# Layer norms of a two-layer hybrid decoder step without GpSimd, with an earlier shift, six blocks in the first group and one pool of PSUM banks

## The chip, the cores and the metric

The kernel runs on one core of one Trainium2 chip. The metric is the time of one execution on the device in microseconds (us). The engines are named as the profile names them: PE (TensorE, the matrix products; PEld is its weight load), DVE (VectorE), ACT (ScalarE), POOL (GpSimd) and SP (SyncE, which issues DMAs).

## The reference

One inference step of 320 tokens (256 of a prompt, 8 sequences of 8) through two layers. Each layer is

```python
h = LayerNorm(alpha * x + W_out [GDN(x) | DiffAttn(x) | GLA(x)])
x = LayerNorm(alpha * h + SwiGLU(h))
# _layer_norm:
mu = jnp.mean(xf, -1, keepdims=True)
var = jnp.mean(jnp.square(xf - mu), -1, keepdims=True)
return ((xf - mu) * lax.rsqrt(var + eps) * g + b)
```

D_MODEL is 2048, so a layer norm runs over 16 blocks of 128 features. The three mixers (gated delta rule, differential attention with a paged cache, gated linear attention) take their columns from one input projection. All tensors are fp32, and the dense products are kept near fp32 by splitting both operands.

## The kernel before

**Layout.** Activations are feature-major: 128 features on the partitions, 320 tokens in the free dimension, 16 blocks `m` for the 2048 features. `acc(m)` (line 766) is the fp32 sum of block `m`; its blocks lie in `blkB`, `accq` and `sv`. `xh` and `xl` hold the input of the next product as high and low part.

**Dense products.** Weights come in units of 256 KB, `raw` (128 x 512), by DMA from SP. ACT casts each to its high part `whi` (`conv_hi`), DVE subtracts to get the low part `wlo` (`conv_lo`), four units ahead. One unit holds four 128 x 128 tiles, and each tile is three products on PE: `whi` by `xh`, `whi` by `xl`, `wlo` by `xh`. So a unit is 12 products, and an output block over 16 k-blocks is 48. There are 19392 dense products in all. A layer has, in this order: the input projection (54 blocks in the order of `IN_BLOCKS`, and the small block `sm` with gates), the output projection in two halves of its inputs (`hf` 0 and 1, 16 blocks each), and the SwiGLU in three parts (gate and up blocks, then 16 `dn` blocks per part). The second half, and the third part, add to `acc(m)`.

**Layer norm.** `ln_part` (line 1070) runs when a block of the last half or part is done. For the first four blocks POOL sums them into `c`, a product with a constant turns that into a mean over 512 features, and `c` is subtracted from every block on DVE as a shift near the mean. `ln_acc` then forms the square on ACT, adds block and square to `S1` and `S2` on POOL, and writes g times the block into `xh` and `xl`. The next product starts on these before the statistics are known: `four` (line 894) makes the first four output blocks go together, one k-block at a time over four banks, with two more columns (322 instead of 320) that carry -g and b; their correction follows in `block_value`. Meanwhile `ln_task` takes two products with a constant for mean and mean square, then the reciprocal root `r`, and then for each block subtracts mu on POOL (`ln_scale`), multiplies by `r` on DVE, applies g and b on ACT twice (`xh` and `acc`) and forms `xl` on DVE. A block may be overwritten only when the first group has used its k-block. The fifth output block needs all of them. There are four layer norms: two feed a SwiGLU, one feeds the input projection of layer 1, and the last (`ln_out`, line 1185) writes the result `y`.

**Banks.** PSUM has 8 banks. Banks 0 to 2 (printed as bank_79 to bank_81) are for dense blocks, 3 to 7 (bank_82 to bank_86) for the mixers; a dense block takes a mixer bank only when no dense bank is free in the program as written.

**What sets the order.** The operations are recorded and then put in an order by `Program.order` (line 511), which knows costs and latencies of each engine, keeps dependencies and the order of the dense products, and takes on each engine the operation with the longest tail behind it. The engines then run their lists in order and wait for one another by semaphores. The planner's costs do not include that DVE and POOL slow each other.

Line 671 of the profile is the call that issues every recorded operation, so rows are told apart by tile names. `geng` and `gen` are the memories that temporaries come from (`c`, `S1`, `S2`, squares and corrected blocks among them).

Of the kernel before, what the change touches and what calls it, by code (L numbers as in the profile page):

```python
# [120 lines left out]
class Mem:  # L121
    """columns of one SBUF tile handed out and taken back in program order, longest-free or (fit) smallest first"""
# [58 lines left out]
class Clock:  # L181
    """rough engine times, used only to choose the order in which work is issued"""
# [56 lines left out]
class TagTile:  # L239
    """a tile of a tag, made when its turn comes in the final order"""  # L240
# [5 lines left out]
class LazyAP:  # L246
    """access pattern of a TagTile: a stand-in for shapes, and the steps that lead to the real one"""
# [53 lines left out]
def region(ap):  # L301
    """(memory, first and last partition, [(first column, last column)]) of an access pattern"""
# [38 lines left out]
class Program:  # L341
    """operations as they are asked for, put in another order that keeps what they depend on, then issued"""
# [6 lines left out]
    # ---- dependencies  # L349
# [19 lines left out]
    def epoch(self, key):  # L369
        """a bank begins a new use"""  # L370
# [51 lines left out]
    def _merge(self, g, o, reads, writes, quads):  # L422
        """o runs beside g, in other columns of the array"""
# [86 lines left out]
    # ---- order  # L510
    def order(self):
# [42 lines left out]
        while len(res) < len(ops):  # L554
# [15 lines left out]
            # choose  # L570
# [103 lines left out]
def aps_of(name, a, kw):  # L674
    """(read, written) access patterns of an operation"""
# [43 lines left out]
def emit(nc, pool, psp, T, O, coff, ioff, n_pages):  # L719
# [32 lines left out]
    dense_free = deque(range(ND))  # L752
    mix_free = deque(range(ND, 8))
# [9 lines left out]

    def acc(m):
# [8 lines left out]
    # ---------------------------------------------------------------- helpers  # L773
# [20 lines left out]
    def rsqrt_small(out, v):  # L794
        """out = v ** -0.5 for a few columns"""
# [6 lines left out]
    # ---------------------------------------------------------------- tasks  # L802
# [63 lines left out]
    def bank(n=1):  # L866
        if clk.task.t > clk.t["PE"] + SLACK:
            yield
        while len(mix_free) < n:
            yield WAIT  # L870
        bs = [mix_free.popleft() for _ in range(n)]
# [4 lines left out]
    def fb(*bs):  # L876
        for b in bs:
            mix_free.append(b)
# [9 lines left out]
    # ---------------------------------------------------------------- units  # L888
# [5 lines left out]
    def four(W, u, keys, ln):  # L894
        """four output blocks, all of them one k at a time; x is not normalized yet where ln is given"""
        for k in range(KB):
            mms = [(keys[m], k, m * 128, k == 0, k == KB - 1) for m in range(4)]
            units.append(dict(src=W[u + k], mms=mms, x=xs2 if ln else xs, n=NT + 2 if ln else NT,
                              pre=("ln" if ln else "x", ln, k)))
        lazy.update({keys[m]: ln for m in range(4) if ln})  # L900

    def one(W, u, key, nk, x, pre=None):
        """one output block over nk k-blocks, four at a time"""
# [5 lines left out]
    def in_units(l):  # L909
# [3 lines left out]
        four(W, 0, keys, ln)  # L913
        u = KB
        for m in range(4, len(keys)):
            u = one(W, u, keys[m], KB, xs, ("h", ln) if ln and m == 4 else None)
            if m == 4:
# [10 lines left out]
    def ffn_units(l):  # L928
        W, W2 = T["wgu"][l], T["wd"][l]
        u = d = 0  # L930
        for pi, (f0, nf) in enumerate(FPARTS):
            keys = [("gu", l, f, gu) for f in range(f0, f0 + nf) for gu in range(2)]
            ms = 0
            if pi == 0:
                four(W, 0, keys, (l, 0))
                u, ms = KB, 4
            for m in range(ms, len(keys)):
                u = one(W, u, keys[m], KB, xs, ("h", (l, 0)) if pi == 0 and m == 4 else None)
# [26 lines left out]
    # ---------------------------------------------------------------- weight stream  # L965
# [1637 lines left out]
```

## Time and profile before

| | |
|---|---|
| median of 3 runs | 3383.41 us (3383.02 to 3388.16) |
| span of the profiled execution | 3386.1 us |
| PE busy | 3292.8 us (97%) |
| DVE busy | 1976.8 us (58%) |
| ACT busy | 1484.9 us (44%) |
| POOL busy | 596.7 us (18%) |
| mean granted TensorE clock | 0.990 |

The time of the profiled execution is not among the three given apart from its span; the span lies 2.7 us above the median and inside the range of the runs. Products overlap (a row of 0.31 us starts 0.15 us after the one ahead), so the pace of PE is read from starts and counts, not from durations. A row with xN joins N like instructions that follow one another.

### The profile page before, as it was taken

How to read it: one execution, taken by the hardware profiler on the slowest of the kernel's cores; microseconds unless marked ns; L12 is line 12 of the kernel's file. 1: busy time of each engine (PE TensorE's matmuls, PEld its weight loads, DVE VectorE, ACT ScalarE, POOL GpSimd, SP SyncE). 2: the span in 40 equal slices, each digit the busy share in tenths (PEclk: the TensorE clock that was granted, in tenths of full speed). 3: DMA queues.
4: the chain of work that ended last, by engine and by line, in shares of the span. 5: the costliest groups of instructions: out<-in, count | busy, mean ns of one | idle time of the engine just before them, and what ended most of it. 6: DMA issues, size and time to landing. Idle time of an engine off the chain costs nothing. (4 is left out here: it accounts for less than half of the span.)

```text
span 3386.1 us, 70352 instructions
## 1 busy us (share of the span) xinstructions
PE 3292.8 (97%) x26570; PEld 3101.2 (92%) x26570; DVE 1976.8 (58%) x3624; ACT 1484.9 (44%) x3059; POOL 596.7 (18%) x825
## 2 busy tenths in 40 slices
PE   9999999999999999999999999999899999999996
PEld 8888787889999999999988887878899999999996
DVE  6666448786445444444876664587954454444446
ACT  5444444445433443344564443453644334433443
POOL 0233423260000000000523333231600000000005
PEclk9999999999999999999999999999999999999998
DMA  6455753434454554544444567434344545454443
GB/s 217 140 175 184 243 189 123 138 118 147 150 150 150 151 150 150 150 150 150 146 145 139 177 213 242 155 116 153 118 147 150 150 150 152 151 150 150 150 150 109
DMA packets 264696, 527.89 MB, mean 156 GB/s; under 512 B 31394, under 2 KB 33570, under 8 KB 264226
## 3 DMA queue, kind: packets, MB, share of 16 engines
q1 hardware_dynamic: 243874, 456.26, 43.8%
q0 software_dynamic: 20480, 67.13, 6.0%
q8 instruction: 208, 3.41, 0.4%
q14 instruction: 134, 1.10, 0.1%
HBM read 506.25 MB, written 16.36 MB: 154 GB/s over the span
## 5 line engine op out<-in xcount | busy, mean ns | idle before, releaser
L671 DVE TENSOR_TENSOR wlo<-raw,whi 128x512 fp32r<-128x512 f32 x1616 | 1166.8, 723 | 1152.9 <-PE bank L671 950.9
L671 ACT CAST whi<-raw 128x512 fp32r<-128x512 f32 x1616 | 999.7, 620 | 1443.2 <-PE bank L671 1351.1
L671 PE MATMUL bank<-xh,whi 128*128 128x320 f32 (+1 forms) x4544 | 1423.0, 313 | 22.3 <-DVE geng L671 10.3
L671 PE MATMUL bank<-xh,wlo 128*128 128x320 f32 (+1 forms) x4544 | 1424.4, 313 | 7.6 <-DVE wlo L671 7.6
L671 PE MATMUL bank<-xl,whi 128*128 128x320 f32 (+1 forms) x4544 | 1420.9, 313 | 0.1
L671 PEld LDWEIGHTS bank<-xh,whi 128*128 128x128 f32 x4544 | 860.4, 189 | 37.9 <-DVE geng L671 11.1
L671 PEld LDWEIGHTS bank<-xh,wlo 128*128 128x128 f32 x4544 | 862.5, 190 | 15.7 <-DVE wlo L671 10.1
L671 PEld LDWEIGHTS bank<-xl,whi 128*128 128x128 f32 x4544 | 860.3, 189 | 15.5 <-issue 11.8
L671 POOL TENSOR_TENSOR geng<-blkB 128x320 f32<-128x320 f32 x8 | 8.1, 1009 | 1747.8 <-DVE blkB L671 1747.8
L671 PE MATMUL bank<-actA,whi 128*128 128x320 f32 x1152 | 254.9, 309 | 0.0
L671 PEld LDWEIGHTS bank<-actA,whi 128*128 128x128 f32 x1152 | 192.7, 188 | 0.0
L671 PE MATMUL bank<-actA,wlo 128*128 128x320 f32 x576 | 177.9, 309 | 0.0
L671 PE MATMUL bank<-actB,whi 128*128 128x320 f32 x768 | 171.2, 310 | 0.0
L671 PE MATMUL bank<-actCh,whi 128*128 128x320 f32 x448 | 138.4, 309 | 0.0
L671 PE MATMUL bank<-actCl,whi 128*128 128x320 f32 x448 | 138.4, 309 | 0.0
L671 PE MATMUL bank<-actCh,wlo 128*128 128x320 f32 x448 | 138.4, 309 | 0.0
L671 PEld LDWEIGHTS bank<-actB,whi 128*128 128x128 f32 x768 | 128.6, 188 | 0.6
L671 PE MATMUL bank<-actB,wlo 128*128 128x320 f32 x384 | 118.9, 310 | 0.1
L671 PE MATMUL bank<-geng,gen 128*32 128x256 f32 (+5 forms) x968 | 109.0, 468 | 5.7 <-DMA geng<-in_ck 4.9
L671 PEld LDWEIGHTS bank<-actA,wlo 128*128 128x128 f32 x576 | 108.3, 188 | 0.0
L671 PEld LDWEIGHTS bank<-g 32*32 32x32 f32 (+2 forms) x2784 | 56.1, 111 | 40.4 <-issue 34.6
L2003 POOL DMA_DIRECT2D geng<-in_cvp x128 | 69.4, 542 | 121.4 <-PE bank L671 100.7
(297 smaller groups left out, 3621.8 us busy)
## 6 DMA issues: line engine op xcount, KB each, us to landing
raw<-in_wgu SPq DMA_DIRECT2D x704, 256.0 KB
raw<-in_win SPq DMA_DIRECT2D x434, 256.0 KB
raw<-in_wd SPq DMA_DIRECT2D x352, 256.0 KB
geng<-in_ck POOLq DMA_DIRECT2D x128, 256.0 KB, 3.9
geng<-in_cvp POOLq DMA_DIRECT2D x128, 256.0 KB, 3.8
raw<-in_wout SPq DMA_DIRECT2D x128, 256.0 KB
c<-in_sgdn SPq DMA_DIRECT2D x6, 512.0 KB
out_gs<-c SPq DMA_DIRECT2D x6, 512.0 KB
```

The source lines that it names most:

```text
L671: fn(*[real(x) for x in a], **{k: real(v) for k, v in kw.items()})
L2003: G.eng.dma_start(out[:, k * 512:k * 512 + 512], src[l, ds(reg, 1)].rearrange(pat))
```

## The change

- The shift moves one part ahead: `ln_shift` runs in the last half but one or part but one (output projection: half 0; SwiGLU: part 1), and `ln_part` in the last one finds blocks that are already shifted.
- All sums and subtractions of the layer norms go from POOL to DVE. `ln_scale`, and the difference for `xl`, work on two blocks at once (128 x 640), and so does the output: `ln_out` uses DVE for both steps, ACT for all 16 affine steps, and 8 DMAs of 320 KB.
- The first group has six output blocks instead of four (`first` instead of `four`, 24 units instead of 16); two `dk` blocks move into it, and the small block comes behind the seventh block instead of the fifth.
- Outside the stretch from the small block to the second half of the output projection (`widen`), all eight banks are one pool that is taken in turn, for dense blocks and mixers alike.

```diff
+FIRST = 6
 IN_BLOCKS = (
     [("dv", h) for h in range(4)]
+    + [("dk", h) for h in (2, 3)]
     + HALF[0]
     + [("dq", h) for h in range(4)]
-    + [("dk", h) for h in range(4)]
+    + [("dk", h) for h in (0, 1)]
...
-    dense_free = deque(range(ND))
-    mix_free = deque(range(ND, 8))
+    dense_free, mix_free = deque(range(8)), deque()
+    wide = [True]
+
+    def widen(on):
+        wide[0] = on
+        old = list(dense_free) + list(mix_free)
+        dense_free.clear()
+        mix_free.clear()
+        for b_ in old:
+            free_dense(b_)
...
     def free_dense(bi):
-        if bi < ND:
+        if wide[0] or bi < ND:
             dense_free.append(bi)
...
+    def first(W, u, keys, ln):
+        todo = [(k, m) for k in range(KB) for m in range(FIRST)]
+        for q in range(len(todo) // 4):
+            km = todo[4 * q:4 * q + 4]
+            mms = [(keys[m], k, i * 128, k == 0, k == KB - 1) for i, (k, m) in enumerate(km)]
...
+            else:
+                widen(True)
...
         if "sm" in u:
+            widen(False)
             small_block(i, u["sm"])
...
+    def ln_shift(ln, m):
+        st = LN
+        if m == 0:
+            st.clear()
+            st["c"] = al(NT)
+            return
         c = ap(st["c"])
         if m < 4:
             if m == 1:
-                tt(G, c, acc(0), acc(1), ALU.add)
+                tt(V, c, acc(0), acc(1), ALU.add)
             elif m > 1:
-                tt(G, c, c, acc(m), ALU.add)
+                tt(V, c, c, acc(m), ALU.add)
             if m == 3:
...
                 for mm_ in range(4):
-                    ln_acc(ln, mm_)
+                    tt(V, acc(mm_), acc(mm_), c, ALU.subtract)
         else:
-            ln_acc(ln, m)
+            tt(V, acc(m), acc(m), c, ALU.subtract)
...
-        tt(V, a, a, c, ALU.subtract)
...
-                tt(G, S1, S1, a, ALU.add)
-            tt(G, S2, S2, sq, ALU.add)
+                tt(V, S1, S1, a, ALU.add)
+            tt(V, S2, S2, sq, ALU.add)
...
-    def ln_scale(m, e):
-        """t -> (t - mu) r"""
-        a = acc(m)
-        tt(e, a, a, ap(LN["S1"]), ALU.subtract)
-        tt(V, a, a, ap(LN["S2"]), ALU.mult)
+    def ln_scale(m):
+        a = acc2(m)
+        for s, op in (("S1", ALU.subtract), ("S2", ALU.mult)):
+            tt(V, a, a, ap(LN[s])[:, None, :].to_broadcast([128, 2, NT]), op)
...
+        for q in (m, m + 1):
+            g, b = pv(l, o + q, 1), pv(l, o + 16 + q, 1)
+            A.activation(xh[:, q, 0:NT], acc(q), AF.Identity, scale=g, bias=b)
+            A.activation(acc(q), acc(q), AF.Identity, scale=g, bias=b)
+        tt(V, xl[:, m:m + 2, 0:NT], acc2(m), f32(xh[:, m:m + 2, 0:NT]), ALU.subtract)
...
     def ln_out(l):
         yield from ln_final(True)
...
+        for m in range(0, KB, 2):
+            ln_scale(m)
+            for q in (m, m + 1):
+                A.activation(acc(q), acc(q), AF.Identity, scale=pv(l, 104 + q, 1), bias=pv(l, 120 + q, 1))
+            SP.dma_start(O["y"][:, m:m + 2, :], acc2(m))
...
-        last = part == (1 if kind == "out" else 2)
-        if last:
-            ln = (l, 0 if kind == "out" else 1)
+        last = 1 if kind == "out" else 2
+        ln = (l, 0 if kind == "out" else 1)
+        if part == last - 1:
+            ln_shift(ln, m)
+        if part == last:
             ln_part(ln, m)
```

**Where the order changes, 1.** PE at the step from the output projection of layer 0 (`oCh`, `oCl`) to the first group of its SwiGLU (`xh`, `xl`, 322 columns). Before, and then the change:

```order
3680 L671 MATMUL bank_80<-oCl_7667,whi 128x320
3681 L671 MATMUL bank_80<-oCh_7304,wlo 128x320
3682 L671 MATMUL bank_81<-xh,whi 128x322
3683 L671 MATMUL bank_81<-xl,whi 128x322
3684 L671 MATMUL bank_81<-xh,wlo 128x322
3685 L671 MATMUL bank_79<-xh,whi 128x322
3686 L671 MATMUL bank_79<-xl,whi 128x322
3687 L671 MATMUL bank_79<-xh,wlo 128x322
3688 L671 MATMUL bank_80<-xh,whi 128x322
```

```order
3698 L673 MATMUL bank_80<-xh,wlo 128x322
3699 L673 MATMUL bank_85<-xh,whi 128x322
3700 L673 MATMUL bank_85<-xl,whi 128x322
3701 L673 MATMUL bank_85<-xh,wlo 128x322
3702 L673 MATMUL bank_83<-xh,whi 128x322
3703 L673 MATMUL bank_83<-xl,whi 128x322
3704 L673 MATMUL bank_84<-geng,cst 128x320
3705 L673 MATMUL bank_82<-geng,cst 128x320
3706 L673 MATMUL bank_83<-xh,wlo 128x322
3707 L673 MATMUL bank_86<-xh,whi 128x322
3708 L673 MATMUL bank_86<-xl,whi 128x322
```

Before, the seventh product of the first group needs bank_80, in which the last block of the projection was summed six products earlier. Now the group begins at row 3690 with banks 81 and 79, and the last block's bank is bank_86, which the group needs first at row 3707, with 15 dense products between; behind 14 of them stand the two products of the statistics (`geng,cst`).

**Where the order changes, 2.** DVE in that first group, where mu and r are applied (`blkB<-blkB,geng`) and `xl` is formed. Before, and then the change:

```order
906 L671 TENSOR_TENSOR blkB<-blkB,geng 128x320
907 L671 TENSOR_TENSOR wlo<-raw,whi 128x512
908 L671 TENSOR_TENSOR blkB<-blkB,geng 128x320 x2
909 L671 TENSOR_TENSOR wlo<-raw,whi 128x512
910 L671 TENSOR_TENSOR blkB<-blkB,geng 128x320
911 L671 TENSOR_TENSOR xl<-blkB,xh 128x320
912 L671 TENSOR_TENSOR blkB<-blkB,geng 128x320
913 L671 TENSOR_TENSOR wlo<-raw,whi 128x512
```

```order
932 L673 TENSOR_TENSOR blkB<-blkB,geng 128x640
933 L673 TENSOR_SCALAR geng<-geng 128x320
934 L673 TENSOR_TENSOR blkB<-blkB,geng 128x640
935 L673 TENSOR_TENSOR wlo<-raw,whi 128x512
936 L673 TENSOR_TENSOR blkB<-blkB,geng 128x640
937 L673 TENSOR_TENSOR wlo<-raw,whi 128x512
938 L673 TENSOR_TENSOR accq_7297<-accq_7297,geng 128x640
```

Before, DVE only multiplies, one block at a time, while POOL subtracts. Now DVE does both for two blocks at a time, and the subtractions stand ahead of the last steps of `r`.

**Where the order changes, 3.** DVE at the end of the program, from the last eviction to `y`. Before, and then the change:

```order
2564 L671 TENSOR_TENSOR sv<-bank_79,sv 128x320
2565 L671 TENSOR_TENSOR sv<-sv,geng 128x320
2566 L671 TENSOR_TENSOR geng<-bank_86,geng 128x320
2567 L671 TENSOR_TENSOR blkB<-blkB,geng 128x320
2568 L671 TENSOR_SCALAR geng<-geng 128x320
2569 L671 TENSOR_TENSOR blkB<-blkB,geng 128x320 x2
2570 L671 TENSOR_TENSOR accq_24555<-accq_24555,geng 128x320 x2
2571 L671 TENSOR_TENSOR geng<-geng 128x320 x2
2572 L671 TENSOR_SCALAR geng<-geng 128x320
2573 L671 TENSOR_TENSOR geng<-geng 128x320
2574 L671 TENSOR_TENSOR blkB<-blkB,geng 128x320 x3
2575 L671 TENSOR_SCALAR blkB<-blkB,prm 128x320
```

```order
2733 L673 TENSOR_TENSOR geng<-bank_80,geng 128x320
2734 L673 TENSOR_TENSOR blkB<-blkB,geng 128x640
2735 L673 TENSOR_SCALAR geng<-geng 128x320
2736 L673 TENSOR_TENSOR blkB<-blkB,geng 128x640 x2
2737 L673 TENSOR_TENSOR accq_24515<-accq_24515,geng 128x640 x2
2738 L673 TENSOR_TENSOR geng<-geng 128x320
2739 L673 TENSOR_TENSOR accq_24515<-accq_24515,geng 128x640
2740 L673 TENSOR_TENSOR geng<-geng 128x320
2741 L673 TENSOR_TENSOR sv<-sv,geng 128x640
2742 L673 TENSOR_SCALAR geng<-geng 128x320
2743 L673 TENSOR_TENSOR sv<-sv,geng 128x640
2744 L673 TENSOR_TENSOR geng<-geng 128x320
```

Before, the last eviction is row 2564, and row 2573 finishes `r`. In the change the last eviction is row 2732, the one ahead of these rows. The subtraction of the shift behind it (row 2565) is gone, the eight wide subtractions come ahead of `r` (row 2744), and behind it stand only the eight wide multiplications; the four affine steps that DVE did for ACT (`blkB,prm` and the like) are gone.

## Rows read from the trace of the kernel before

**Rows 1.** The page: span and busy time of the engines.

```profile
span 3386.1 us, 70352 instructions
PE 3292.8 (97%) x26570; PEld 3101.2 (92%) x26570; DVE 1976.8 (58%) x3624; ACT 1484.9 (44%) x3059; POOL 596.7 (18%) x825
```

**Rows 2.** Busy time by stretch: PE, PEld, DVE, ACT, POOL, granted clock, DMA share, GB/s.

```profile
700.00:800.00 100.00, 88.73 (x552) 84.91 (x551) 87.64 (x136) 62.01 (x122) 46.08 (x42) 0.95 0.41 123
800.00:1600.00 800.00, 800.00 (x5464) 800.00 (x5463) 369.04 (x587) 315.35 (x537) 0.00 (x0) 1.00 0.50 150
1600.00:1725.00 125.00, 118.93 (x799) 116.24 (x801) 105.91 (x155) 72.87 (x140) 55.60 (x51) 0.99 0.45 136
2375.00:2475.00 100.00, 88.69 (x551) 84.83 (x550) 89.23 (x137) 62.04 (x121) 48.97 (x44) 0.95 0.40 119
```

**Rows 3.** PE's waits from 700 to 800 us: total, times, longest.

```profile
PE bank L671 <- DVE wlo L671: 3.9, 4, 1.4
PE bank L671 <- DVE sv L671: 3.5, 2, 2.6
PE bank L671 <- DVE geng L671: 3.4, 1, 3.4
```

**Rows 4.** Timeline of PE, 738 to 777 us: start, duration, [idle before, releaser].

```profile
738.42 0.64 PE L671 MATMUL bank<-xh,whi 128*128 128x322 f32 x1 [2.63 <-DVE sv L671]
...
740.20 0.47 PE L671 MATMUL bank<-xh,whi 128*128 128x322 f32 x1
740.47 0.47 PE L671 MATMUL bank<-xl,whi 128*128 128x322 f32 x1
...
776.40 0.41 PE L671 MATMUL bank<-xh,whi 128*128 128x320 f32 x1 [3.42 <-DVE geng L671]
```

**Rows 5.** Timeline of DVE, 737 to 765 us.

```profile
737.89 0.48 DVE L671 TENSOR_TENSOR sv<-bank,sv 128x320 f32<-128x320 f32 x1
...
760.77 1.16 DVE L671 TENSOR_TENSOR blkB<-blkB,geng 128x320 f32<-128x320 f32 x1
761.86 1.16 DVE L671 TENSOR_TENSOR xl<-blkB,xh 128x320 fp32r<-128x320 f32 x1
...
763.34 0.68 DVE L671 TENSOR_TENSOR wlo<-raw,whi 128x512 fp32r<-128x512 f32 x1
763.94 0.48 DVE L671 TENSOR_TENSOR blkB<-blkB,geng 128x320 f32<-128x320 f32 x1
764.35 0.48 DVE L671 TENSOR_TENSOR xl<-blkB,xh 128x320 fp32r<-128x320 f32 x1
```

**Rows 6.** Timeline of POOL in the same stretch.

```profile
758.12 4.55 POOL L671 TENSOR_TENSOR sv<-sv,geng 128x320 f32<-128x320 f32 x4
```

**Rows 7.** Timeline of ACT: the affine steps at 775 us.

```profile
775.00 0.64 ACT L671 ACTIVATE xh<-sv,prm 128x320 fp32r<-128x320 f32 x1
775.54 0.64 ACT L671 ACTIVATE accq<-accq,prm 128x320 f32<-128x320 f32 x1
```

**Rows 8.** Timelines of DVE and ACT behind the last dense product, to the end.

```profile
3358.93 0.49 DVE L671 TENSOR_TENSOR sv<-bank,sv 128x320 f32<-128x320 f32 x1 [5.33 <-PE bank L671]
3359.46 0.49 DVE L671 TENSOR_TENSOR sv<-sv,geng 128x320 f32<-128x320 f32 x1
3361.48 0.49 DVE L671 TENSOR_TENSOR geng<-bank,geng 128x320 f32<-128x320 f32 x1 [1.53 <-PE bank L671]
...
3368.77 0.49 DVE L671 TENSOR_TENSOR geng<-geng 128x320 f32<-128x320 f32 x1
...
3381.60 0.65 ACT L671 ACTIVATE sv<-sv,prm 128x320 f32<-128x320 f32 x1 [0.53 <-DVE sv L671]
```

**Rows 9.** Busy time by stretch, as rows 2: the first half of the output projection.

```profile
590.00:675.00 85.00, 81.73 (x552) 69.87 (x550) 68.31 (x117) 36.58 (x87) 20.07 (x16) 0.98 0.43 136
```

**Rows 10.** PE's waits from 100 to 700 us, two of nine.

```profile
PE bank L671 <- DVE gen L671: 5.4, 6, 1.6
PE bank L671 <- DMA c<-in_sgdn: 2.1, 1, 2.1
```

More of the change, by code (lines that the diff above doesn't have):

```diff
@@ L868, in bank @@
             yield
-        while len(mix_free) < n:
+        while len(dense_free if wide[0] else mix_free) < n:
             yield WAIT
-        bs = [mix_free.popleft() for _ in range(n)]
+        bs = [(dense_free if wide[0] else mix_free).popleft() for _ in range(n)]
         for b_ in bs:
@@ L877, in fb @@
         for b in bs:
-            mix_free.append(b)
+            free_dense(b)
     def until(*fl):
@@ L892, in emit @@
     xs2 = lambda k: (xh[:, k, :], xl[:, k, :])
[L894 to L900, printed above, removed]
+    def first(W, u, keys, ln):
[3 more added lines that the diff above has]
+            mms = [(keys[m], k, i * 128, k == 0, k == KB - 1) for i, (k, m) in enumerate(km)]
+            new = [k for k, m in km if m == 0]
+            units.append(dict(src=W[u + q], mms=mms, x=xs2 if ln else xs, n=NT + 2 if ln else NT,
+                              pre=("ln" if ln else "x", ln, new[0]) if new else None,
+                              used=[(ln, k) for k, m in km if m == FIRST - 1]))
+        lazy.update({keys[m]: ln for m in range(FIRST) if ln})
+        return u + len(todo) // 4
     def one(W, u, key, nk, x, pre=None):
@@ L912, in in_units @@
         ln = (l - 1, 1) if l else None
[L913 to L917, printed above, removed]
+        u = first(W, 0, keys, ln)
+        for m in range(FIRST, len(keys)):
+            u = one(W, u, keys[m], KB, xs, ("h", ln) if ln and m == FIRST else None)
+            if m == FIRST:
                 units.append(dict(src=W[u], sm=("in", l, "sm", 0)))
@@ L934, in ffn_units @@
             if pi == 0:
-                four(W, 0, keys, (l, 0))
-                u, ms = KB, 4
+                u, ms = first(W, 0, keys, (l, 0)), FIRST
             for m in range(ms, len(keys)):
-                u = one(W, u, keys[m], KB, xs, ("h", (l, 0)) if pi == 0 and m == 4 else None)
+                u = one(W, u, keys[m], KB, xs, ("h", (l, 0)) if pi == 0 and m == FIRST else None)
             for m in range(16):
@@ L1044, in emit_unit @@
             step()
-        if pre and pre[0] == "ln":
-            set_flag(("used", pre[1], pre[2]))
+        for ln, k in u.get("used", ()):
+            if ln:
+                set_flag(("used", ln, k))
     def small_block(i, key):
@@ L1074, in ln_part @@
             st["c"] = al(NT)
+            return
+        c = ap(st["c"])
+        if m < 4:
+            if m == 1:
+                tt(V, c, acc(0), acc(1), ALU.add)
+            elif m > 1:
+                tt(V, c, c, acc(m), ALU.add)
+            if m == 3:
+                b = (dense_free or mix_free).popleft()
+                prog.epoch(f"bank{b}")
+                mm(banks[b][:, 0:NT], cs("i512").to_broadcast([128, 128]), c)
+                A.copy(c, banks[b][:, 0:NT])
+                free_dense(b)
+                for mm_ in range(4):
+                    tt(V, acc(mm_), acc(mm_), c, ALU.subtract)
+        else:
+            tt(V, acc(m), acc(m), c, ALU.subtract)
+    def ln_part(ln, m):
+        st = LN
+        if m == 0:
+            fr(st["c"])
             st["S1"] = al(NT)
@@ L1173, in ln_task @@
         set_flag(("lnst", ln))
-        ln_scale(0, G)
-        for m in range(KB):
+        ln_scale(0)
+        for m in range(0, KB, 2):
             clk.task.t = flags[("lnst", ln)]
-            yield from until(("used", ln, m))
-            if m + 1 < KB:
-                ln_scale(m + 1, G)
+            yield from until(("used", ln, m), ("used", ln, m + 1))
+            if m + 2 < KB:
+                ln_scale(m + 2)
             ln_affine(ln, m)
             set_flag(("h", ln, m))
+            set_flag(("h", ln, m + 1))
             yield
@@ L2494, in tiles, with first @@
         return w[:, m * 128:(m + 1) * 128].reshape(w.shape[0] // 128, 128, 128)
-    def four(out, blocks):
-        out[0:KB] = np.stack(blocks, 0).transpose(1, 2, 0, 3).reshape(KB, 128, 512)
-        return KB
+    def first(out, blocks):
+        w = np.stack(blocks, 1).reshape(-1, 4, 128, 128)
+        out[0:len(w)] = w.transpose(0, 2, 1, 3).reshape(-1, 128, 512)
+        return len(w)
     def one(out, u, blk):
@@ L2514, in pack @@
             bl.append(t.reshape(KB, 128, 128))
-        u = four(win[l], bl[:4])
-        u = one(win[l], u, bl[4])
+        u = first(win[l], bl[:FIRST])
+        u = one(win[l], u, bl[FIRST])
         t = np.zeros((KB, 128, 32), np.float32)
@@ L2521, in pack @@
         u += 1
-        for b in bl[5:]:
+        for b in bl[FIRST + 1:]:
             u = one(win[l], u, b)
```

59 lines of the change are left out of this document (10 added, 49 removed).

## The prediction

> **What bounds the kernel now.** I read the page first, then busy time by stretch, then PE's waits in the stretches where PE falls behind, then the timelines there. The page says that PE works 97% of the span [rows 1], so only what PE loses can be won, and the end of the program. Where PE never waits, from 800 to 1600 us, 5464 products take 800 us, 0.1464 us each [rows 2]. Against that pace the three stretches around the first three layer norms lose: 700 to 800 us holds 552 products, worth 80.8 us, so 19.2 us are lost; 2375 to 2475 us holds 551, so 19.3 are lost; 1600 to 1725 us holds 799, worth 117.0, so 8.0 are lost. Together 46.5 us. The fourth layer norm ends the program: the last eviction starts at 3358.93 and the span ends at 3386.1 [rows 1, 8].
>
> Between 700 and 800 us PE waits 3.9 us for `wlo`, 3.5 for `sv` and 3.4 for `geng`, all from DVE [rows 3]; the third stretch reads alike. The `sv` waits are for banks: the first group's seventh product needs the bank of the projection's last block, and DVE reads that bank only at 737.89, so PE goes on at 738.42 [rows 4, 5]. The `geng` wait is the fifth output block, whose bank holds the first block of the group until DVE has corrected it. Both waits of about 3 us are followed by slow products: 0.27 us apart at 740 us instead of 0.146 [rows 4], the lower of the two clock levels, and the mean granted clock of the stretch is 0.95 [rows 2].
>
> Why DVE is late stands in its timeline. At 760.77 us a step on one block starts 1.09 us before its successor; at 763.94 the same step takes 0.41, and a `wlo` 0.60 [rows 5]. What differs is POOL: its run of subtractions, 1.14 us each, starts at 758.12 and ends at 762.67 [rows 6]. The evictions, which read a bank and one tile, stay at 0.48 us, as at 737.89.
>
> **The change, part by part.** Durations are of the profiled execution, span 3386.1 us, 2.7 above the median of 3383.41; I take the sum off both.
>
> *Sums and subtractions from POOL to DVE, shift one part earlier.* In the last half of an output projection a block of 24 products lasts 3.5 us. DVE then has two `wlo` (1.2), the eviction (0.4), two sums (0.8) and `xl` (0.4): 2.8 us, and nothing beside it on POOL. It keeps up, which ends the `wlo` waits there.
>
> *Six blocks and wide steps.* The first group grows from 192 products, 28.1 us, to 288, 42.2 us. In it DVE has 24 `wlo` (14.4), sixteen steps on two blocks, eight wide `xl`, the steps of `r` (some 2.5) and the first two corrections (1.7). A wide step is not in the trace; from 0.40 for 320 and 0.60 for 512 columns I estimate 0.75 for 640, with 0.80, two single steps, as the upper bound. That makes 12.0, 6.0 and a sum of 36.6 us: under 42.2, where before the wait came. ACT has 24 casts and 32 affine steps at 0.54 us [rows 7], 30 us at most, and also fits. The two more columns on 96 products cost 0.1 us.
>
> *Eight banks in turn.* The last block's bank is used again after 15 products instead of six, and the seventh and eighth output block take the two banks that the statistics leave. Both bank waits go. Late next are the statistics: they stand behind 14 products, 2.05 us, while DVE needs for eviction, a `wlo` and two sums some 1.9 us and the start of the chain besides. I charge 0.4 us of waiting and 1.1 for the two fp32 products, 1.5 per stage: of 46.5 lost, 42.0 are won. The bounds are 21 (half the losses stay) and 46.5. In the rest of the dense work PE shows no wait [rows 2], so eight banks bring nothing there.
>
> *The shift in the first half of the output projection.* There it lands beside the mixers' last work: DVE is busy 68.3 of 85 us, POOL 20 [rows 9]. Nineteen more steps on DVE cost 7.6 us at 0.40, or 20.7 at the stretched 1.09; 16.7 are free. So per layer the cost lies between nothing and 4 us; I take 1.5, since POOL works a quarter of the time. For two layers 3.0, bound 8. In the SwiGLU's second part DVE is half idle [rows 2], and it costs nothing.
>
> *The small block two blocks later.* The gated mixers start 96 products, 14.1 us, later in each layer, and the first group keeps six banks from the attention. By the order the mixers' other products have caught up with the dense ones well before the input projection ends: ahead of the first product of the output projection stand 2592 dense and 1789 other products in either version. I charge nothing; the cover is the dense work of that projection. If it were gone, 28.2 us would be lost. The mixers' own waits, such as 5.4 us for `gen` and 2.1 for a state's DMA [rows 10], will fall elsewhere; I allow 5 us either way.
>
> *The end.* The subtraction of the shift between last eviction and statistics goes, 0.53 us [rows 8]. From 3360.95 (3361.48 less 0.53) DVE does eight wide subtractions (6.0) and the steps of `r` (some 2.3): `r` is ready at 3369.2, as before at 3369.26. Then a wide multiplication, 0.75, and ACT's 16 affine steps at 0.54, 8.7 us, which now set the pace: 3378.8 with the handover. Before, the last ended at 3382.25 [rows 8]. That is 3.45 us, less some 0.5 since the last DMA moves 160 KB more: an estimate from 150 GB/s at half of the DMA engines' time [rows 2]. 3.0 won, bounds 1 and 4.5.
>
> The Trainium skill, Perfetto Trace Analysis, section Optimizing Scalar/DVE Operations, speaks against the wide steps here: it advises grouping where an engine is saturated, but breaking up where Scalar or Vector are not and others wait for them. No run here shows both forms. By that rule single steps would start ACT 0.35 us sooner and halve the last DMA, so the end would come 0.8 us earlier than in the sum above; the sum itself stands, as ACT's 16 steps take the same time either way.
>
> Sum: 42.0 + 3.0 - 3.0 = 42.0 us. From 3386.1 that gives 3344.1, from the median 3341.4.
>
> **The rivals.**
> *DVE becomes the bound where POOL was (0.15).* The three stages then keep half their losses, by statistics that hold up PE and by the clock behind them. For it: the margin at the statistics is nil by my sum, and PE runs in order. Against: 36.6 of 42.2 us. It wins 21 instead of 42: about 3362.
> *The mixers gain too (0.08).* Their order is new, and the waits of [rows 10] happen to close: 10 us more, 3331.
> *The mixers lose (0.08).* The late small block holds back the chain of the gated delta rule for a third of the 28.2 us: 3351.
> *Slower (0.05).* In the first half of the output projection DVE with 19 more steps beside POOL makes each `wlo` late, PE stops again and again, and the clock falls. A stop there costs as the two measured ones do, some 3 us and 14 products at 0.12 us more, 4.7 us. Nine of them over both layers eat the 42 us, from eleven on the kernel is over 0.2% slower: about 3391. For it: DVE already works 80% there. Against: 16.7 us of DVE are free.
> That the change doesn't do what it says is no rival: the order shows the POOL steps gone and the banks in turn.
>
> **How the numbers follow.** My forecast has 0.64, with its own range of 3334 to 3350 from the bounds of the projection's first half, the end and the mixers. The range for 8 in 10 takes in the mixers' cases and most of the first rival's: 3329 to 3364. Faster by over 0.2% (6.8 us, about what a measurement of this kernel tells from no change) hold all but the last case, less a little for halved gains that meet a loss in the mixers: 0.92. Within 0.2%: 0.03. Slower: 0.05.
>
> **What would show it.** Right: around the three layer norms PE's pace stays near 0.1464 us and the granted clock 1.00; no waits for `sv` or for a corrected block; DVE steps of 0.40 where POOL is silent; the last affine step some 20 us behind the last eviction instead of 23. Wrong: waits of PE for `geng` at the statistics, `wlo` waits in the first half of the output projection, or a longer stretch from 60 to 700 us.

## The result, and the profile after

The changed kernel takes 3332.51 us (median; 3331.14 to 3335.01), beside 3383.22 us for the kernel before in the same rounds: a ratio of 0.9849, 95% interval 0.9835 to 0.9863. That is 50.7 us less, where 42.0 were forecast; 3332.5 lies in the range of 3329 to 3364, 8.5 us under the forecast of 3341. The profiled execution spans 3331.3 us.

The page of the changed kernel, span and busy time of the engines:

```profile
span 3331.3 us, 69934 instructions
PE 3271.5 (98%) x26570; PEld 3088.4 (93%) x26570; DVE 1966.5 (59%) x3734; ACT 1491.0 (45%) x3069; POOL 389.1 (12%) x634
```

Against [rows 1] POOL loses a third of its work, and yet DVE, which took over that work, is busy 10 us less. Busy time by stretch of the changed kernel, columns as in [rows 2]:

```profile
700.00:800.00 100.00, 100.00 (x677) 99.69 (x676) 82.71 (x146) 68.62 (x130) 1.16 (x2) 1.00 0.54 153
800.00:1600.00 800.00, 800.00 (x5462) 799.84 (x5461) 382.60 (x617) 317.71 (x543) 0.00 (x0) 1.00 0.54 150
1600.00:1725.00 125.00, 125.00 (x863) 123.01 (x862) 96.66 (x179) 79.53 (x157) 3.97 (x12) 1.00 0.54 153
2338.00:2438.00 100.00, 100.00 (x677) 99.68 (x676) 86.88 (x155) 70.69 (x132) 0.00 (x0) 1.00 0.53 148
```

The stage around the first layer norm holds 677 products in 100 us where it held 552; 677 at 0.1464 us are worth 99.1, so 0.9 us are lost where 19.2 were. The third, with its window moved to where the stage now lies, reads the same, and the granted clock is 1.00 in all of them. The second now holds 863 products in 125 us, where a pace of 0.1464 us gives 854: some of them are shorter products of the mixers. From 680 to 1760 us the trace has not one wait of PE: all lines of [rows 3] are gone. DVE's timeline in the first group:

```profile
750.37 0.82 DVE L673 TENSOR_TENSOR xl<-blkB,xh 128x640 fp32r<-128x640 f32 x1
751.11 0.82 DVE L673 TENSOR_TENSOR accq<-accq,geng 128x640 f32<-128x640 f32 x1
751.84 0.69 DVE L673 TENSOR_TENSOR wlo<-raw,whi 128x512 fp32r<-128x512 f32 x1
...
762.27 0.69 DVE L673 TENSOR_TENSOR wlo<-raw,whi 128x512 fp32r<-128x512 f32 x1 [1.13 <-PE bank L673]
```

A step on two blocks starts 0.74 us before its successor, less than one block took beside POOL in [rows 5] (1.09). From 762 us on DVE waits for PE, so it is no longer what is late. The end, DVE and then ACT, as in [rows 8]:

```profile
3307.56 0.49 DVE L673 TENSOR_TENSOR sv<-bank,sv 128x320 f32<-128x320 f32 x1 [4.77 <-PE bank L673]
...
3317.14 0.48 DVE L673 TENSOR_TENSOR geng<-geng 128x320 f32<-128x320 f32 x1
...
3322.08 1.55 DVE L673 TENSOR_TENSOR sv<-sv,geng 128x640 f32<-128x640 f32 x2
```

```profile
3318.51 3.38 ACT L673 ACTIVATE blkB<-blkB,prm 128x320 f32<-128x320 f32 x6 [6.47 <-DVE blkB L673]
3321.80 3.36 ACT L673 ACTIVATE accq<-accq,prm 128x320 f32<-128x320 f32 x6
3325.07 2.27 ACT L673 ACTIVATE sv<-sv,prm 128x320 f32<-128x320 f32 x4
```

ACT's last affine step ends at 3327.34, 19.8 us behind the start of the last eviction, and DVE is done 3.7 us before it.

**Where the time came from.** Starts of products that both versions have cut the two profiled executions (3386.1 and 3331.3 us) into pieces; a second profiled execution of the changed kernel (run `d0_changed_again`, 3325.2 us) shows how far the pieces scatter.

| from, to | before | after | after, again |
|---|---|---|---|
| start, first product of output projection 0 | 590.7 | 590.8 | 587.0 |
| to its second half | 83.3 | 82.7 | 82.0 |
| to the first group behind the second layer norm | 1005.1 | 985.9 | 985.9 |
| to the output projection of layer 1 (with its mixers) | 588.8 | 578.9 | 577.4 |
| to the first group behind the third layer norm | 144.5 | 137.7 | 137.4 |
| to the last dense product | 946.2 | 931.4 | 931.4 |
| to the end | 27.5 | 24.1 | 24.1 |

Dense pieces repeat to 0.3 us; those with mixers differ by up to 4 us between executions of one kernel. The same scatter is in all medians below, so 1 to 4 us are read from pieces and not from medians. One more piece serves for that: from the first product of a first group to the 600th dense product behind it, the changed kernel takes 89.6, 97.7 and 89.6 us in the first three stages, and the same again in its second execution.

### The profile page after: what moved, and what is told of

Its sections match the earlier page's. It is cut to its first block, busy times and chain, and to the rows that moved or that the text cites. A ratio compares the mean times of both kernels' runs of the same rounds, so it can differ in the third digit from the quotient of the medians.

```text
span 3331.3 us, 69934 instructions
## 1 busy us (share of the span) xinstructions
PE 3271.5 (98%) x26570; PEld 3088.4 (93%) x26570; DVE 1966.5 (59%) x3734; ACT 1491.0 (45%) x3069; POOL 389.1 (12%) x634
## 4 chain that ended last, share of the span: by engine, by line
PE 91%; DVE 3%; DMA 2%; issue 2%; ACT 1%; POOL 0%; POOLq 0%; SPq 0%; ACTq 0%; DVEq 0%
PE bank L673 91%; DVE gen L673 1%; DVE wlo L673 1%; DMA geng<-in_ck 1%; DMA gen<-in_sgdn 0%; DMA c<-in_sgdn 0%; DVE geng L673 0%; SPq L673 0%; POOLq L2012 0%; DMA out_gs<-gen 0%; POOL geng L673 0%; DMA out_gs<-c 0%; ACT geng L673 0%; DVE blkB L673 0%; DMA raw<-in_win 0%
## 5 line engine op out<-in xcount | busy, mean ns | idle before, releaser
L673 DVE TENSOR_TENSOR wlo<-raw,whi 128x512 fp32r<-128x512 f32 x1616 | 1126.9, 698 | 1110.8 <-PE bank L673 903.3
L2014 POOL DMA_DIRECT2D geng<-in_ck x128 | 70.3, 550 | 242.6 <-DVE actA L673 130.9
```

The source lines that it names most:

```text
L673: fn(*[real(x) for x in a], **{k: real(v) for k, v in kw.items()})
L2014: G.eng.dma_start(out[:, k * 512:k * 512 + 512], src[l, ds(reg, 1)].rearrange(pat))
```

## The experiments

Theory: what DVE has to do around the statistics was too long, mostly since POOL's work beside it stretched its steps. Rivals: the banks, the longer group, or the early shift carry the gain. Four kernels take back one part of the change each, three add one part alone to the kernel before; two put idle work on POOL. The steps on two blocks, the new end and the later small block were not taken back by themselves.

| kernel | median us | against the changed kernel (3332.5) or before (3383.6) |
|---|---|---|
| changed, again | 3333.1 | +0.6 |
| changed, three dense banks | 3331.7 | -0.8 |
| changed, four blocks in the group | 3341.5 | +9.0 |
| changed, sums and mean on POOL | 3352.1 | +19.6 |
| changed, late shift | 3328.0, again 3331.8 | -4.5, -1.3 beside its own repeat |
| before, no POOL | 3355.8 | -27.8 |
| before, eight banks | 3370.6 | -13.1 |
| before, six blocks | 3363.5 | -20.1 |
| changed, idle additions on POOL | 3340.0 | +7.5 |
| changed, idle fills on POOL | 3335.2 (2 runs) | +2.6 |

**One part taken back.** Three banks for dense work throughout:

```diff
-    dense_free, mix_free = deque(range(8)), deque()
-    wide = [True]
+    dense_free, mix_free = deque(range(ND)), deque(range(ND, 8))
+    wide = [False]
```

(and the two calls of `widen` are gone)

> The changed kernel with one part undone: dense work keeps three banks and the mixers five throughout, as before. Theory (POOL's leaving makes most of the gain, and the banks a smaller part of their own): the sv wait of 2.6 us at the group's seventh product and the geng wait of 3.4 us behind the group come back in the two SwiGLU stages, each with slow products behind it, some 10 us a stage, and little in the stage of the input projection: 15 to 22 us above the changed kernel, so 3348 to 3354. Rival (banks carry the gain): 35 us or more, above 3367. Rival (with DVE early, three banks are enough): under 4 us, below 3337.

Measured 3331.73 us, ratio to before 0.9843 (0.9824 to 0.9863), and no wait of PE from 700 to 800 us. The third expectation holds: with DVE early, three banks and the mixers' five are enough.

Four blocks in the first group (`FIRST = 4` and the old order of the input blocks):

> The changed kernel with one part undone: the first group holds four output blocks again, all else stays. Theory: DVE's work behind the statistics (some 36 us by the old sum, without the correction of two blocks 32) no longer fits under 28 us of products, so the first product behind the group waits some 4 to 6 us in each of three stages, with slow products behind it: 15 to 25 us above the changed kernel, 3347 to 3357. Rival (cover carries the gain, since then as before PE stands twice): 35 us or more. Rival (early shift and DVE steps alone fit under four blocks): under 4 us.

Measured 3341.51 us, 0.9880 (0.9862 to 0.9898): under the theory's 15 to 25. To the 600th dense product the first three stages are 3.3, 3.0 and 3.3 us longer than in the changed kernel, all of it behind the group of four, which takes 29.4 us. PE's waits there, 700 to 800 us:

```profile
PE bank L672 <- DVE xl L672: 1.1, 1, 1.1
PE bank L672 <- ACT whi L672: 0.8, 1, 0.8
PE bank L672 <- DVE wlo L672: 0.2, 1, 0.2
```

The waits are short, and the granted clock of the stretch stays at 1.00, so the slow products that were charged behind them did not come: that was the part over-charged.

Sums and mean on POOL again:

```diff
-                tt(V, S1, S1, a, ALU.add)
-            tt(V, S2, S2, sq, ALU.add)
+                tt(G, S1, S1, a, ALU.add)
+            tt(G, S2, S2, sq, ALU.add)
```

(and likewise the sums for `c` and the subtraction of mu, one block at a time)

> The changed kernel with one part undone: the sums of the shift and of the statistics and the subtraction of the mean run on POOL again (one block at a time, 1.14 us each), six blocks, banks and the early shift stay. Theory (POOL beside DVE stretches DVE's steps from 0.40 to 1.09 us and delays wlo and the statistics): most of the loss of the three stages returns, 25 to 46 us above the changed kernel, 3357 to 3378; DVE steps near 1.09 us again, wlo waits of PE again. Rival (longer cover and more banks hide a late DVE): under 8 us, below 3341, with the stretched steps in the trace and no PE waits.

Measured 3352.07 us, 0.9913 (0.9891 to 0.9934): the largest of the four, between both expectations. DVE's steps on two blocks take 1.49 us while POOL subtracts, and PE waits 2.1 us for `wlo` in the group, which lasts 47.2 us instead of 43.7. To the 600th dense product the three stages are 3.4, 3.3 and 3.4 us longer, 10.1 together; some 7 and 5.5 more come in the first halves of the two output projections. There PE's product for the shift (`gen,cst`) waits for POOL's last sum into `c`, which lies in `gen` here. PE's waits, 600 to 680 us, then that product and that sum:

```profile
PE bank L673 <- POOL gen L673: 3.1, 1, 3.1
PE bank L673 <- DVE gen L673: 0.5, 1, 0.5
```

```profile
625.92 0.81 PE L673 MATMUL bank<-gen,cst 128*128 128x320 f32 x2 [3.11 <-POOL gen L673]
623.88 1.98 POOL L673 TENSOR_TENSOR gen<-gen,blkB 128x320 f32<-128x320 f32 x1 [4.89 <-DVE blkB L673]
```

POOL itself had waited for DVE's block, and its sum takes 1.98 us. So with the sums on POOL the early shift stops PE, and the granted clock of 590 to 675 us is 0.94, where the changed kernel has 0.98 and, in its second execution, 1.00. This part of the 19.6 us belongs to POOL's sums and the early shift together.

The shift in the last part, all on DVE:

```diff
-        if part == last - 1:
-            ln_shift(ln, m)
         if part == last:
-            ln_part(ln, m)
+            ln_shift(ln, m)
+            if m > 2:
+                for q in range(4) if m == 3 else (m,):
+                    ln_part(ln, q)
```

(and `c` is given back later)

> The changed kernel with one part undone: the shift is taken in the last part again (sums of four blocks, a product, and a subtraction on each block there), all on DVE. Theory: one more DVE step of 0.40 us per block of 3.5 us in a part where DVE has 2.8 us of work: it still keeps up but for the first blocks, the tail gets 0.5 us back, so 0 to 6 us above the changed kernel, 3332 to 3339. Rival (the early shift is what frees DVE ahead of the statistics): 12 us or more above, with wlo waits of PE in the last parts.

Measured 3328.03 us, 0.9834 (0.9815 to 0.9853): no loss at all, against the sign of the theory. Its profiled execution is 4.9 us earlier already at the first product of output projection 0, ahead of everything in which the two kernels differ, so it was run again beside the changed kernel.

> The changed kernel itself, once more, on the chip and in the rounds of the next two, so that differences of 1 to 5 us can be told from the scatter of the runs. Both theories: 3329 to 3336.

> The changed kernel with the shift taken in the last part throughout, once more, with five rounds. Theory (the early shift costs some 1 us in the first half of each output projection, the late one 0.5 us at the end; the other 3 us of the first comparison were scatter of the mixers): 1 to 3 us under the changed kernel run beside it. Rival (the early shift costs all of the 4.5 us that the first comparison showed): 4 us or more under it.

Measured 3333.09 us (0.9856, 0.9840 to 0.9872) and 3331.82 us (0.9845, 0.9828 to 0.9862): the medians do not tell them apart. By the pieces, an output projection takes 137.3 and 137.5 us with the late shift in layer 0, 138.1 and 137.4 with the early one; in layer 1 136.6 and 136.9 beside 137.7 and 137.4. So the early shift costs at most 1 us in each output projection, first and second half taken together, and gives 0.6 us back at the end (24.7 beside 24.1).

**One part alone.** No POOL (the sums, and mu, on DVE in the kernel before):

> The kernel before with one part of the change alone: the sums of the shift and of the statistics and the subtraction of the mean go from POOL to DVE, one block at a time; four blocks, three banks and the late shift stay. Theory (what DVE must do around the statistics has to fit under the group's products, and POOL's leaving is what shortens it most): the wlo waits and the stretched steps go; the sv and geng waits of banks stay in part: 25 to 38 us under before, 3345 to 3358. Rival (any one part alone is given back by the next wait, only parts together win): under 12 us, above 3371, with sv and geng waits as long as before.

Measured 3355.80 us, 0.9923 (0.9907 to 0.9940), inside the theory's range. From 700 to 800 us:

```profile
PE bank L671 <- DVE xl L671: 1.7, 5, 0.7
PE bank L671 <- ACT whi L671: 0.8, 2, 0.5
PE bank L671 <- DVE wlo L671: 0.4, 2, 0.2
```

The `sv` and `geng` waits of [rows 3] are gone without a bank more: they were DVE's lateness. Why it was late ahead of the statistics shows in two of its steps for a block of the last half, in the kernel before and then in this one:

```profile
725.75 1.06 DVE L671 SCALAR_TENSOR_TENSOR xl<-accq,prm,xh 128x320 fp32r<-128x320 f32 x1
726.73 1.36 DVE L671 TENSOR_TENSOR wlo<-raw,whi 128x512 fp32r<-128x512 f32 x1
```

```profile
718.74 0.55 DVE L671 SCALAR_TENSOR_TENSOR xl<-accq,prm,xh 128x320 fp32r<-128x320 f32 x1
719.60 0.69 DVE L671 TENSOR_TENSOR wlo<-raw,whi 128x512 fp32r<-128x512 f32 x1
```

In the kernel before POOL adds beside these steps, from 725.26 to 727.55 us; here it does nothing. What stays is a group of four that is too short: behind it, from 757 to 767 us, PE stops nine times for 0.2 to 0.7 us, and from 766.7 to 772.9 us its products are slow. The stretch holds 615 products at a mean granted clock of 0.97, where three stops, the longest 1.1 us, left it at 1.00 with four blocks above. How much of the 27.8 us was stretched steps and how much waiting for POOL's own results was not separated in the kernel before.

Eight banks:

> The kernel before with one part of the change alone: all eight banks in turn outside the mixers. Theory (a bank is waited for only because DVE is late, as undoing the banks in the changed kernel cost nothing): the sv wait of some 2.6 us goes in two stages and the loss moves to DVE's steps behind it: 0 to 12 us under before, 3371 to 3383. Rival (the bank waits and the slow products behind them are most of the loss): 20 us or more, below 3363.

Measured 3370.59 us, 0.9965 (0.9951 to 0.9979), 13.1 us under before and so just past the theory's 12. PE's waits from 700 to 800 us, the three longest:

```profile
PE bank L671 <- POOL geng L671: 4.5, 1, 4.5
PE bank L671 <- DVE wlo L671: 2.7, 4, 1.1
PE bank L671 <- DVE xl L671: 0.7, 2, 0.4
```

The `sv` and DVE's `geng` wait go, but a longer one comes: the statistics, which stand behind 23 products here, wait 4.5 us for POOL's last sum, which itself had waited 1.6 us for DVE. This is the place of the first rival in the prediction, with DVE and POOL late one behind the other.

Six blocks:

> The kernel before with one part of the change alone: six output blocks in the first group, with POOL, three banks for dense work and the late shift as before. Here the group's blocks beyond the third take their banks from the mixers' part. Theory (cover and a shorter DVE each make up for the other): the wait behind the group goes and the sv wait at its head stays or grows: 10 to 25 us under before, 3358 to 3373. Rival (without POOL's leaving a longer group is of no use, DVE and POOL just run as late): under 6 us. Rival (cover alone does it all): 35 us or more, below 3348.

Measured 3363.51 us, 0.9938 (0.9922 to 0.9955), as the theory said: the `geng` wait behind the group goes, and the others stay as they were.

```profile
PE bank L673 <- DVE wlo L673: 4.0, 4, 1.4
PE bank L673 <- DVE sv L673: 3.5, 2, 2.6
```

Alone the three parts (no POOL, eight banks, six blocks) win 27.8, 13.1 and 20.1 us, 61.0 together, more than the 50.7 of the change (the early shift was not run alone). Taken back they cost 19.6, nothing and 9.0. They stand in for each other.

**Idle work on POOL.** Nobody reads its results, so only its presence is tried:

```diff
+        for _ in range(n):
+            tt(G, junk, src, cs("cos"), ALU.add)
```

> The changed kernel with 48 additions more on POOL in each of the first three layer norms, 128x320 each, on finished xl blocks and constants into a scratch tile that nobody reads: POOL is as busy beside DVE as before, but nobody waits for its results. Theory (POOL's work by itself stretches DVE's steps): in the group of six blocks DVE's steps on two blocks last 1.2 us or more instead of 0.74 wherever POOL works, and PE's stage is longer by 3 us or so, as with the sums on POOL: 5 to 15 us above the changed kernel. Rival (DVE was late because it waited for POOL's results, the steps were long for that reason): steps stay at 0.74, time within 4 us of the changed kernel.

Measured 3340.00 us, 0.9878 (0.9862 to 0.9895). To the 600th dense product the three stages are 3.3, 0.8 and 3.5 us longer than in the changed kernel, 7.6 together, as much as the medians differ. POOL and DVE of this kernel:

```profile
752.87 2.50 POOL L673 TENSOR_TENSOR geng<-xl,cst 128x320 f32<-128x320 f32 x2 [2.16 <-DVE xl L673]
757.53 4.95 POOL L673 TENSOR_TENSOR geng<-xl,cst 128x320 f32<-128x320 f32 x4 [2.17 <-DVE xl L673]
```

```profile
739.41 0.82 DVE L673 TENSOR_TENSOR sv<-sv,geng 128x640 f32<-128x640 f32 x1
...
752.65 0.81 DVE L673 TENSOR_TENSOR sv<-sv,geng 128x640 f32<-128x640 f32 x1
753.38 1.25 DVE L673 TENSOR_TENSOR wlo<-raw,whi 128x512 fp32r<-128x512 f32 x1
754.55 1.50 DVE L673 TENSOR_TENSOR sv<-sv,geng 128x640 f32<-128x640 f32 x1
755.97 0.68 DVE L673 TENSOR_TENSOR wlo<-raw,whi 128x512 fp32r<-128x512 f32 x1
756.58 0.81 DVE L673 TENSOR_TENSOR xl<-blkB,xh 128x640 fp32r<-128x640 f32 x1
```

The same step takes 0.82 us at 739.41, where POOL is silent from 731.6 to 748.2, and 1.50 at 754.55, with no dependency between them. (Step by step the match is rough: the row at 752.65 begins before POOL's and is not stretched, the one at 754.55 outlasts it.) The stretched sums make PE wait for the statistics in the first and third stage:

```profile
727.72 1.34 PE L673 MATMUL bank<-geng,cst 128*128 128x320 f32 x4 [3.02 <-DVE geng L673]
```

The other kernel of the pair fills the scratch tile four times, behind an addition of 8 columns, in place of each addition:

> The changed kernel with idle work on POOL in the first three layer norms that hardly reads: in place of each of the 48 additions one of 8 columns and four fills of 128x320 of the scratch tile. Theory (two-operand work on POOL holds back DVE's two-operand steps by reading and writing the same memory ports): fills, which only write, stretch DVE's wide steps less than the additions did (1.50 us beside POOL, 0.82 alone): 0.82 to 1.1 us, time within 4 us of the changed kernel. Rival (any work on POOL stretches DVE's steps as long as it lasts): 1.4 us or more.

Measured 3335.15 us, 0.9860 (0.9839 to 0.9881). DVE, and POOL beside it:

```profile
753.91 0.81 DVE L673 TENSOR_TENSOR sv<-sv,geng 128x640 f32<-128x640 f32 x1
754.64 0.68 DVE L673 TENSOR_TENSOR wlo<-raw,whi 128x512 fp32r<-128x512 f32 x1
755.24 0.82 DVE L673 TENSOR_TENSOR sv<-sv,geng 128x640 f32<-128x640 f32 x1
```

```profile
753.36 1.63 POOL L673 MEMSET geng<- 128x320 f32 x4
755.07 0.31 POOL L673 TENSOR_TENSOR geng<-xl,cst 128x8 f32<-128x8 f32 x1
755.44 1.64 POOL L673 MEMSET geng<- 128x320 f32 x4
```

POOL is busy 40 of the 50 us from 725 to 775, and DVE's steps last as long as without it; the stage keeps its 677 products from 700 to 800 us, and all three stages are as long as in the changed kernel to 0.1 us. So it is neither POOL's work as such nor what it writes, but additions, which read two tiles; other work that reads was not tried.

**A version meant to be faster** takes the shift late in the output projections only, and gives DVE four of the last 16 affine steps (the lines that move the shift are not shown):

```diff
-                A.activation(acc(q), acc(q), AF.Identity, scale=pv(l, 104 + q, 1), bias=pv(l, 120 + q, 1))
+                g, b = pv(l, 104 + q, 1), pv(l, 120 + q, 1)
+                if q in (7, 11, 13, 15):
+                    tsc(V, acc(q), acc(q), g, ALU.mult, b, ALU.add)
+                else:
+                    A.activation(acc(q), acc(q), AF.Identity, scale=g, bias=b)
```

> A version meant to be faster: the shift is taken in the last half of the output projections and, as in the change, in the second part of the SwiGLU; at the end DVE takes four of ACT's 16 affine steps. Theory: some 1 us per output projection, and at the end ACT's 12 steps take 6.7 us behind r instead of 8.9, with DVE done about then too: last affine step some 17.7 us behind the last eviction instead of 19.8; in all 3 to 4 us under the changed kernel. Rival (the end waits for the transfers of y or for DVE, whose steps now stand in the way): no gain at the end, 0 to 2 us.

Measured 3327.91 us, 0.9837 (0.9820 to 0.9853). It beats the kernel before; its 5.2 us on the changed kernel beside it are less than the two intervals can tell apart. The end shows what it won:

```profile
3306.25 0.49 DVE L673 TENSOR_TENSOR sv<-bank,sv 128x320 f32<-128x320 f32 x1 [4.77 <-PE bank L673]
...
3322.95 0.80 DVE L673 TENSOR_SCALAR sv<-sv,prm 128x320 f32<-128x320 f32 x2
```

```profile
3322.68 1.19 ACT L673 ACTIVATE sv<-sv,prm 128x320 f32<-128x320 f32 x2
```

The last affine step ends 17.6 us behind the last eviction, 2.2 earlier, as expected, but the span ends only 1.2 earlier (22.9 us behind the last dense product, before 24.1): the other 1.0 us goes behind the issues of `y`. The eight now come in 5.9 us instead of 8.0, and the span ends 4.9 us behind the start of the last one, in the changed kernel 4.0. Whether smaller transfers would end sooner was not tried. The output projections are 1.3 and 0.9 us shorter than in the changed kernel's two executions on average.

## Why the prediction was right, point by point

The mechanism was right: the waits, the slow products and the stretched steps around the layer norms went, and they are most of the gain. The gain was 8.7 us more than forecast. The measured 3332.5 lies 1.5 us under the forecast's own range of 3334 to 3350, inside the wider one, and nearest to the rival that the mixers gain too (3331). Where the rest came from is told piece by piece.

**The layer norms** (46.5 us lost, 42.0 to be won). Right in kind, and a little more was there than forecast. The 1.5 us kept per stage were 0.9, with no wait at the statistics; the 0.4 charged for one there did not come. The 8.0 us lost in the second stage were under-read, since the count of products took in shorter ones of the mixers. By like products the three stages gave 18.8, 8.4 and 19.0 us, 46.2 together: each taken from the start of the second half of the output projection (before the second layer norm, the last 600 dense products) to the 600th dense product of the next stage (in the second, the 200th, as the mixers come in behind it). The forecast of 0.75 us for a step on two blocks was 0.74.

**Which part does what.** The prediction priced the stages as a whole, and that came out. Its reason why both bank waits go was one of two: eight banks alone remove them, but then PE waits for the statistics; POOL's leaving alone removes them too, and undoing the banks in the changed kernel costs nothing.

**The shift in the first half of the output projection** (1.5 a layer charged). The charge was near. The half takes 81.6 to 82.9 us in layer 0 and 81.8 to 82.8 in layer 1 in six executions with the early shift on DVE (the changed kernel twice, three banks, four blocks, both kernels with idle work); in three with the late shift (that kernel twice, and the last version) it takes 80.5 to 81.5 and 80.6 to 80.9. On the mean the early shift costs 1.1 and 1.5 us there, and the second half gives 0.5 back (55.4 beside 56.0). DVE works 74.07 us of 85, beside 68.31 in [rows 9], and PE's waits have no `wlo` among them. What the prediction did not have is that this half would shrink all the same: against the kernel before it is 0.6 to 1.3 us shorter in layer 0 and 2.6 to 2.9 in layer 1. The rival that ends slower had this place; its nine stops did not come. The run with the sums on POOL shows that the place is real: there PE did stop, 3.1 us at a time, for POOL.

**The small block later, and the mixers** (nothing, 5 us either way). The first piece of the table is the same within its scatter. From 100 to 700 us PE's waits sum to 15.8 us before and 15.6 after: in layer 0 they moved, and did not shrink. The piece with layer 1's mixers also holds 7.4 us of the second stage; it gains 10.0 and 11.5, so 2.6 to 4 us are the mixers' or unread, inside the 5 allowed. In the output projections PE's waits for `gen`, a temporary of the mixers, fall from 3.3 to 1.2 us in layer 0 and from 3.3 to 1.7 in layer 1. That their new order closed these waits was not tried by itself, and it is not all: without POOL in the kernel before, the first half in layer 0 takes 82.1 us with its `gen` waits at 3.3. Why the first halves shrank stays open.

**The end** (3.0). 3.4 us; last affine step 19.8 us behind the last eviction where some 20 were forecast, and ACT sets the pace, as said.

**The sum by pieces**, forecast and then read from the two executions: first half of output projection 0, -1.5 and 0.6; to the group behind the second layer norm, 17.7 and 19.2; to the output projection of layer 1, 6.5 and 10.0; on to the last dense product, 16.3 (17.8 less 1.5 for the shift) and 21.6; the end, 3.0 and 3.4. That is 42.0 and 54.8. Of the 12.8 us more, 6.2 lie in the first halves of the output projections (3.0 charged, 3.2 won), 4.2 in the three stages, 2.6 in the rest of the piece with layer 1's mixers and 0.4 at the end; 0.6 are lost elsewhere. Between the medians the change is worth 50.7 and not 54.8, so 4.1 us of this belong to the two executions that were profiled. The kernel before has one trace only, so it can't be said in which piece they lie; the pieces with mixers are those that scatter.

**The rival that DVE becomes the bound** did not come: DVE waits for PE at the end of the group. It is what the kernels with POOL's sums or with four blocks turn into, in part. The advice of the Trainium skill (Perfetto Trace Analysis, section Optimizing Scalar/DVE Operations) to break steps up, which the prediction set against the wide steps, was not tried.

## What to carry to other kernels

When several waits follow one another around one step, price the group and not each wait: here any one of three parts won 13 to 28 us alone, and two of the three were worth half or nothing once the others were in. Ask of each wait which engine was late, and what ran beside it: here a wait for a bank was a late VectorE, whose steps additions on GpSimd had stretched. Taking work over from an engine that seems free need not lengthen the engine that takes it: VectorE was busy 10 us less in all.

## What the runs showed of the hardware

Additions on POOL nearly double DVE's steps with two operands in SBUF (0.81 to 1.50 us for 128x640; 0.68 to 1.25 for `wlo`), while they themselves are held up less: 1.07 us on the mean of all 144, 1.24 in the run of four above, and 0.87 at 739.78 us in the kernel before, where DVE stands idle to 740.49. Fills do not touch those steps. The Trainium skill says the same in SBUF — State Buffer, section Who interferes with whom: a VectorE step with two SBUF inputs contends with GpSimd work that reads SBUF, and not with work that only writes it. These runs agree and add the size. A step that reads a bank and one tile keeps its duration: 0.48 us at 737.89 in [rows 5], beside a POOL addition from 737.58 to 738.68. A step with one input in SBUF, the one with two constants that leads to `r`, took 0.54 us beside a fill, 1.01 beside additions (at 730.76 us in the kernel with idle additions, where POOL adds from 729.28 to 731.58), and 0.32 in the changed kernel. Beside the fill:

```profile
740.67 0.54 DVE L673 TENSOR_SCALAR geng<-geng 128x320 f32<-128x320 f32 x1
```

Whether slow products follow a stop of PE does not go by its length alone. In the kernel before, stops of 2.6 and 3.4 us were followed by products some 0.27 us apart (at 740 us, [rows 4], and from 777.7 to 781.1), the lower of the two clock levels. The 3.0 us before the statistics beside idle additions, and the 2.1 us with the sums on POOL, were not: the granted clock from 700 to 800 us is 1.00 in both. In the kernel before without POOL, slow products came behind nine stops of at most 0.7 us. So a stop is not worth the same everywhere, as the prediction's 4.7 us had it.

One kernel's two executions differ by 3.7 us before the first output projection, in the mixers, where its dense stages repeat to 0.3.
